# Gate and up products: three 256-column matmuls per block become one of 512 and one of 256 columns, and POOL takes two scalings and the last product

## The chip, the cores and the metric

The kernel runs on one core of a Trainium2 chip. The metric is the device time of one execution in microseconds (us). Each core has TensorE (PE; its weight loads are listed apart as PEld), VectorE (DVE), ScalarE (ACT), GpSimd (POOL) and SyncE (SP), which here only issues DMAs. Every engine works through its own queue in order, and an instruction that waits holds up all that stand behind it on that engine.

## The reference

Two layers of a decoder on x (256 tokens, 1024 features, float32). The change lies in the second half of a layer, the gated ConvFFN on RMSNorm(x):

```python
def conv_ffn(h, w_gate, w_up, conv_w, conv_b, w_down):   # h = rms_norm(x, ln2): [256, 1024]
    g = h @ w_gate                                        # w_gate, w_up: [1024, 2816]
    u = h @ w_up
    g = causal depthwise convolution of g, width 3, + conv_b
    return (silu(g) * u) @ w_down                         # w_down: [2816, 1024]
```

## The kernel before

Activations lie with features on the 128 partitions and the 256 tokens along the free axis. Float32 precision is kept by splitting: each operand is a high half and a low half (`hi`, `lo` for weights; `hTh`, `hTl` for h; `aTh`, `aTl` for the gated product), and a product is three matmuls in the function `mm3` (lines 195 to 197): high by high, high by low, low by high.

**Weights.** All weights pass through one stream in the order of their use. SP loads 1 MiB into a raw buffer; for each half MiB (a part) `split_next` puts a rounding copy on ACT (`hi`, line 180) and a subtraction on DVE (`lo`, line 181). Seven pairs of split buffers form a ring, and `weights()` keeps up to six parts split ahead of PE. So ACT and DVE do one `hi` and one `lo` for each part that PE uses, and a `hi` waits until PE has finished the part seven places earlier.

**The gate and up stage.** For each of NM = 22 blocks m of 128 hidden features, `products(m)` (line 849) computes gate and up: each has its own part of weights and, for 8 blocks k of the contraction, one `mm3` into a [128, 256] half of a PSUM bank. Banks come from the tags `acc` and `s`, two each, in turn; the block m = 2 uses `o` and `m` instead. `combine(m)` (line 858) then runs on the other engines, with R the norm's factor per token:

1. DVE: gr = gate x R (line 860)
2. ACT: y = conv tap 2 x gr + bias (line 862)
3. DVE: two `scalar_tensor_tensor` add the shifted taps to y (line 864)
4. ACT: s = Silu(y) (line 867)
5. POOL: s = s x R (line 868)
6. DVE: y = up x s (line 869), up still in PSUM
7. ACT: aTh = high half of y (line 870); DVE: aTl = the rest (line 871)

The blocks 0 and 1 are combined together behind the products of block 1, since R is computed (`norm2`, line 841) behind the products of block 0. After the stage, `down` (line 301) multiplies the 22 blocks by w_down; the blocks' results are used there in their order. Which instruction stands where on ACT, DVE and POOL is decided when the program is built, by a scheduler that fills each engine's queue; on the chip that order is fixed.

Of the kernel before, what the change touches and what calls it, by code (L numbers as in the profile page):

```python
# [11 lines left out]
F32 = mybir.dt.float32  # L12
# [8 lines left out]
P = 128  # L21
# [11 lines left out]
# steps of the attention behind each part of a chunk of the input projection, and of the output projection  # L33
# [3 lines left out]
# input projection: chunks of columns in the order in which they are computed  # L37
# [22 lines left out]
# rows of w_out in the order in which the pairs of heads are finished  # L60
# [4 lines left out]
# small per-layer parameters, [128, SMN]  # L65
O_LN1, O_LN2, O_CW, O_CB, O_PEK, O_PEV, SMN = 0, 8, 16, 82, 104, 120, 136
# gain rows
G_QA, G_KA, G_QB, G_KB1, G_KB2, G_QC, G_KC, G_KB0 = range(8)
# constants
# [41 lines left out]
def emit(ctx, tc, a):  # L111
# [22 lines left out]
    hTh = cst.tile([P, 8, S], F32R, name="hTh")  # L134
    hTl = cst.tile([P, 8, S], F32R, name="hTl")
# [7 lines left out]
    # ---- weights: streamed in the order of their use, each split into two 12-bit halves  # L143
    RAWN, SPN, AHEAD = 3, RING, RING - 1
    stream = []  # (source, columns of a part, parts): a part is half of a 1 MiB transfer
# [20 lines left out]
    after = []  # the splits are queued behind these  # L166
# [32 lines left out]
    def rsqrt(out, ss, n, tmp=None):  # L199
        # out = (ss / n + eps) ** -0.5  # L200
        v, w, q = tmp or [sml.tile(list(out.shape), F32, tag=f"rs_{i}", name=f"rs_{i}") for i in "vwq"]
        # a first value by exp(-0.5 ln v), then one step of Newton's method
        V.tensor_scalar(v, ss, 1.0 / n, EPS, ALU.mult, ALU.add)
        A.activation(out=w, in_=v, func=ACTF.Ln)
        A.activation(out=w, in_=w, func=ACTF.Exp, scale=-0.5)
        V.tensor_tensor(q, w, w, ALU.mult)
        V.scalar_tensor_tensor(q, q, -0.5, v, ALU.mult, ALU.mult)
        V.scalar_tensor_tensor(out, q, 1.5, w, ALU.add, ALU.mult)

    def make_h(k, gcol, sqs):  # L210
        # h = x * gain in two halves, without the factor r of the norm; sqs += squares
        g = gcol[:, k:k + 1]
        ins = [A.activation(out=hTh[:, k], in_=xT[:, k], func=ACTF.Copy, scale=g)]
        ins.append(V.scalar_tensor_tensor(out=hTl[:, k], in0=xT[:, k], scalar=g, in1=f(hTh[:, k]), op0=ALU.mult, op1=ALU.subtract))  # L214
        if sqs is not None:
            square(k, sqs)
        return ins

    def square(k, sqs):
        # sqs[0]: the sum of the squares of the tiles 0..k  # L220
# [7 lines left out]
    def factor(out, sqs, tag):  # L228
        # out[token, tile] = (sum of squares / D + eps) ** -0.5
# [6 lines left out]
    # keep the array's clock up while the first loads are under way  # L236
# [4 lines left out]
    # ---- the other loads, each behind a part of the stream  # L241
# [59 lines left out]
    def down(acc, lT, i0, i1, last, done=None, hold=False):  # L301
        # acc[d, tokens] += w^T lT for the parts i0..i1 of the contraction; two tiles of d share a bank
# [9 lines left out]
    for L in range(DEPTH):  # L312
        sm = sms[L]
        with ExitStack() as ph:
# [3 lines left out]
            # ---- the first norm: its factor r is applied to the rows of the projection  # L318
# [18 lines left out]
            def proj(c):  # L337
                # chunk c of the input projection, a part of the contraction at a time
# [21 lines left out]
            def qk_norm(q, groups):  # L360
                # rms norm and rope, in place, of the heads in q[:, t, 0:nh*64]; groups: (first head, heads, gain)
# [21 lines left out]
            def qk_T(z, outs_of):  # L383
                # -> for each group of heads, queries: [128, pair, head of pair, 256], each head's high halves on its own
                # rows (64 * head of pair ...) and its low halves on the other rows; keys: high halves on all rows,
                # [128, head of pair, pair, 256], and low halves on the head's own rows, [128, pair, 256]
# [30 lines left out]
            def qk_T32(z, h0, n, tag):  # L417
                # -> [128, pair, 256]: d of the two heads of a pair on rows 0..63 and 64..127
# [12 lines left out]
            def qk_mm(out, qs, p, k, t, kh, kl):  # L431
                # out = q k^T for the queries of tile t; kh, kl: [128, keys]
# [5 lines left out]
            def softmax(pr, ps, mask, m, nb, den):  # L438
                # pr[i] = exp(0.125 (ps[i] + mask[i] - max)), not normalised; m, nb, den: [P, 1] each
# [13 lines left out]
            def scores(pr, qT, kT, p, k, mk, m, nb, den):  # L453
                # pr: [P, 384] = (queries 0, keys 0), (queries 1, keys 0 and 1); m, nb, den: [P, 2]
# [6 lines left out]
            def scores2(qs, kk, p, k, m, nb, den):  # L461
                # selected and window keys at once: pr[:, branch]; m, nb, den: [P, 4] by (branch, tile)
# [11 lines left out]
            def prob_T(pr, sc):  # L474
                # pr: [P, 384] scaled by sc [P, 2] and transposed
# [5 lines left out]
                # columns: (keys 0, q 0) (keys 0, q 1) (keys 1, q 1)  # L481
# [4 lines left out]
            def pv(pTs, vs, O, first, last):  # L486
                # O[64 k.., q] += v^T p^T for the two heads k of a pair, on the two halves of the array at a time
# [28 lines left out]
            def attention():  # L516
                # the attention of all heads in steps; each yields the chunk of the projection that the next one needs
                yield 0
                gn = gns[L]
                # gains folded into the rope tables  # L520
# [10 lines left out]
                # ---- NSA: compressed keys and values  # L531
                hs = at.tile([P, 2, P], F32, tag="hs", name="hs", bufs=1)
                for i in range(2):
# [3 lines left out]
                    # t2[(parity, d), kv, s] = t[2 s + parity, kv, d]  # L537
# [15 lines left out]
                    # four column groups of the array at a time, each a part of the contraction  # L553
# [13 lines left out]
                # gelu, tanh form: z / (1 + exp(-2 sqrt(2 / pi) (z + 0.044715 z^3)))  # L567
# [12 lines left out]
                for i in range(2):  # L580
# [20 lines left out]
                    if i == 0:  # twice, for both halves of the queries  # L601
                        V.tensor_copy(b, bc(cb, [30, 2, HD]))
                    else:  # each of the two heads on its own columns
                        V.tensor_tensor(b, bc(cb, [30, 2, HD]), bc(bm, [30, 2, HD]), ALU.mult)
                    bd.append(b.rearrange("p h d -> p (h d)"))
                # values and, later, probabilities: high halves on rows 0..29; the high halves again or the low ones on 32..61
# [9 lines left out]
                # kc[:, k]: the high halves on all rows, the low halves on the rows of head k  # L616
# [18 lines left out]
                # compressed attention, all heads at once: [P, tile, pair, member, n]  # L635
# [20 lines left out]
                # gates: heads stand as (pair, member) = head pair + 3 * member  # L656
# [72 lines left out]
                # ---- dilated  # L729
# [12 lines left out]
                # weights of the groups: exp(m_g - M) / sum_g den_g exp(m_g - M)  # L742
# [13 lines left out]
                # ---- MoBA  # L756
# [59 lines left out]
            # ---- output projection  # L816
# [16 lines left out]
        with ExitStack() as ph:  # L833
# [7 lines left out]
            def norm2():  # L841
                # the second norm's factor, along the free dimension on all partitions
# [6 lines left out]
            def products(m):  # L849
                gu = [bank((("acc", "s"), ("o", "m"))[m == 2][i], "ps_gu")[:, :S] for i in range(2)]  # L850
                ws = [weights() for _ in range(2)]
                for ps, (hi, lo) in zip(gu, ws):
                    for k in range(8):
                        cs = slice(k * P, (k + 1) * P)
                        mm3(ps, hi[:, cs], lo[:, cs], hTh[:, k], hTl[:, k], k == 0, k == 7)
                return gu

            def combine(m, g, u):
                gr = ff.tile([P, S], F32, tag="gr", name="gr", bufs=3)
                V.tensor_tensor(gr, g, R, ALU.mult)  # L860
# [7 lines left out]
                G.tensor_tensor(s_, s_, R, ALU.mult)  # L868
                V.tensor_tensor(y, u, s_, ALU.mult)  # L869
# [3 lines left out]
            waiting = []  # L873
            for m in range(NM):
                waiting.append((m, *products(m)))
# [3 lines left out]
                if m >= 1:  # L879
                    for w in waiting:  # L880
                        combine(*w)
                    waiting = []
# [46 lines left out]
def build(arrays):  # L929
    nc = bacc.Bacc("TRN2", target_bir_lowering=False, num_devices=1)  # L930
# [12 lines left out]
```

## Time and profile before

| what | value |
|---|---|
| time, median of 3 runs | 679.56 us (679.25 to 679.63) |
| span of the profiled execution, first to last instruction | 677.8 us |
| the median less that span | 1.8 us |
| mean granted TensorE clock | 0.995 |
| busy: PE, PEld, DVE, ACT, POOL | 98%, 91%, 72%, 58%, 14% |

The profiled execution has its span alone; the median of the runs is 1.8 us longer, which is taken as what lies around a span. Busy time counts an instruction from its start to its end. Matmuls overlap each other, so the distance from one start to the next tells the pace, not the duration that is listed.

### The profile page before, as it was taken

What the parts mean: (1) busy time and instruction counts of PE and PEld (TensorE: products, weight loads), DVE (VectorE), ACT (ScalarE), POOL (GpSimd) and SP (SyncE); (2) the same over time, 40 slices, a digit from 0 to 9 for tenths busy, and PEclk for the clock granted to TensorE, in tenths of its full rate; (3) what the DMA queues carried; (4) which work ended last, traced back from release to release, by engine and by line L of the source; (5) the groups of instructions that cost most, each with busy time, mean ns of one, the idle gap of its engine ahead of it and who ended that gap; (6) DMA issues with size and microseconds to landing.
All of it is one profiled execution on the core that took longest, in us unless ns stands there. A gap on an engine that the chain in (4) does not pass through costs nothing. (4 is left out here: it accounts for less than half of the span.)

```text
span 677.8 us, 12841 instructions
## 1 busy us (share of the span) xinstructions
PE 665.2 (98%) x5062; PEld 617.0 (91%) x5062; DVE 488.0 (72%) x1066; ACT 396.4 (58%) x786; POOL 97.1 (14%) x133
## 2 busy tenths in 40 slices
PE   7999999999999999999989999999999999999997
PEld 6889768889999999999988887687999999999997
DVE  6689877769877777744476898796787777775432
ACT  5467779568555555543365767876765555555320
POOL 6301000112111111100050010010311111110000
PEclk9899999999999999999989999999999999999999
DMA  7956234515555555564745421533265555556501
GB/s 236 375 175 207 82 118 143 187 64 187 167 178 179 178 182 182 184 214 158 239 172 187 151 78 67 187 124 126 68 243 186 180 178 181 180 177 222 190 2 63
DMA packets 19356, 111.84 MB, mean 165 GB/s; under 512 B 2144, under 2 KB 3936, under 8 KB 8288
## 3 DMA queue, kind: packets, MB, share of 16 engines
q1 hardware_dynamic: 19296, 111.02, 48.5%
q8 instruction: 40, 0.66, 0.4%
q14 instruction: 20, 0.16, 0.1%
HBM read 109.97 MB, written 1.05 MB: 164 GB/s over the span
## 5 line engine op out<-in xcount | busy, mean ns | idle before, releaser
L181 DVE TENSOR_TENSOR lo<-raw,hi 128x1024 fp32r<-128x1024 f32 (+3 forms) x212 | 242.3, 1150 | 79.9 <-ACT hi L180 79.0
L180 ACT ACTIVATE hi<-raw 128x1024 fp32r<-128x1024 f32 (+3 forms) x212 | 207.8, 989 | 77.8 <-PE ps_dn L196 50.7
L195 PE MATMUL ps_gu<-hTh,hi 128*128 128x256 f32 x704 | 199.6, 284 | 0.0
L196 PE MATMUL ps_gu<-hTl,hi 128*128 128x256 f32 x704 | 199.4, 283 | 0.1
L197 PE MATMUL ps_gu<-hTh,lo 128*128 128x256 f32 x704 | 199.2, 283 | 0.0
L196 PEld LDWEIGHTS ps_gu<-hTl,hi 128*128 128x128 f32 x704 | 135.1, 192 | 0.5 <-DVE hTl L214 0.5
L195 PEld LDWEIGHTS ps_gu<-hTh,hi 128*128 128x128 f32 x704 | 135.1, 192 | 0.1
L197 PEld LDWEIGHTS ps_gu<-hTh,lo 128*128 128x128 f32 x704 | 135.1, 192 | 0.0
L195 PE MATMUL ps_dn<-aTh,hi 128*128 128x256 f32 x352 | 98.6, 280 | 0.0
L196 PE MATMUL ps_dn<-aTl,hi 128*128 128x256 f32 x352 | 98.2, 279 | 0.0
L197 PE MATMUL ps_dn<-aTh,lo 128*128 128x256 f32 x352 | 98.2, 279 | 0.0
L196 PE MATMUL ps_in<-lo,hTh 128*128 128x384 f32 (+3 forms) x256 | 90.6, 355 | 3.2 <-DVE lo L181 3.2
L195 PE MATMUL ps_in<-hi,hTh 128*128 128x384 f32 (+3 forms) x256 | 90.4, 356 | 0.2 <-ACT hi L180 0.2
L197 PE MATMUL ps_in<-hi,hTl 128*128 128x384 f32 (+3 forms) x256 | 89.4, 350 | 0.0
L197 PEld LDWEIGHTS ps_dn<-aTh,lo 128*128 128x128 f32 x352 | 66.2, 188 | 0.0
L195 PEld LDWEIGHTS ps_dn<-aTh,hi 128*128 128x128 f32 x352 | 66.1, 188 | 0.0
L196 PEld LDWEIGHTS ps_dn<-aTl,hi 128*128 128x128 f32 x352 | 65.8, 187 | 0.0
L196 PEld LDWEIGHTS ps_in<-lo,hTh 128*128 128x128 f32 x256 | 49.3, 193 | 8.3 <-DVE lo L181 4.4
L870 ACT CAST aTh<-cy 128x256 fp32r<-128x256 f32 x44 | 17.9, 407 | 65.7 <-DVE cy L869 65.6
L195 PEld LDWEIGHTS ps_in<-hi,hTh 128*128 128x128 f32 x256 | 49.0, 192 | 6.1 <-issue 2.8
L197 PEld LDWEIGHTS ps_in<-hi,hTl 128*128 128x128 f32 x256 | 49.4, 193 | 3.6 <-issue 1.2
L864 DVE SCALAR_TENSOR_TENSOR cy<-gr,sm,cy 128x255 f32<-128x255 f32 x88 | 42.1, 481 | 2.2 <-ACT cy L862 0.7
(316 smaller groups left out, 930.3 us busy)
## 6 DMA issues: line engine op xcount, KB each, us to landing
raw<-w_gu SPq DMA_DIRECT2D x44, 1024.0 KB, 5.0
raw<-w_down SPq DMA_DIRECT2D x22, 1024.0 KB, 4.8
raw<-w_in SPq DMA_DIRECT2D x16, 768.0 KB, 4.3
raw<-w_in SPq DMA_DIRECT2D x8, 1024.0 KB, 4.9
raw<-w_out SPq DMA_DIRECT2D x8, 1024.0 KB, 4.9
w<-cw SPq DMA_DIRECT2D x4, 1024.0 KB, 8.6
raw<-w_in SPq DMA_DIRECT2D x4, 512.0 KB, 3.7
raw<-w_in SPq DMA_DIRECT2D x4, 274.0 KB, 4.6
```

Source lines behind the costliest of these rows:

```text
L180: A.activation(out=hi[:, :n], in_=r, func=ACTF.Copy)
L181: V.tensor_tensor(out=lo[:, :n], in0=r, in1=f(hi[:, :n]), op=ALU.subtract)
L195: T.matmul(out, lhsT=lh, rhs=rh, start=start, stop=False, skip_group_check=skip)
L196: T.matmul(out, lhsT=lh, rhs=rl, start=False, stop=False, skip_group_check=skip)
L197: T.matmul(out, lhsT=ll, rhs=rh, start=False, stop=stop, skip_group_check=skip)
L864: V.scalar_tensor_tensor(out=y[:, j:], in0=gr[:, :S - j], scalar=cw[:, m, 2 - j:3 - j], in1=y[:, j:], op0=ALU.mult, op1=ALU.add)
L870: A.copy(aTh[:, m], y)
```

## The change

h's two halves move into one tile, so that for each block k the 256 high and the 256 low columns lie side by side. Each `mm3` of the stage becomes two matmuls: the weights' high half against all 512 columns, into both halves of a PSUM bank, and the low half against the 256 high columns, into the first half. For gate and for up, ACT copies the second half of the bank to SBUF, DVE adds the first half, and POOL multiplies by R. The last product y = up x s moves from DVE to POOL and reads SBUF alone; the old scaling of s on POOL goes. All blocks use the banks of `acc` and `s`, and each block is combined right behind its products. A new tile `cu` (three buffers) holds the up product; a scratch area for DMAs is made smaller to give it room.

```diff
-    hTh = cst.tile([P, 8, S], F32R, name="hTh")
-    hTl = cst.tile([P, 8, S], F32R, name="hTl")
+    hT = cst.tile([P, 8, 2, S], F32R, name="hT")
+    hTh, hTl = hT[:, :, 0], hT[:, :, 1]
...
             def products(m):
-                gu = [bank((("acc", "s"), ("o", "m"))[m == 2][i], "ps_gu")[:, :S] for i in range(2)]
+                gu = [bank(t, "ps_gu").rearrange("p (o n) -> p o n", o=2) for t in ("acc", "s")]
                 ws = [weights() for _ in range(2)]
                 for ps, (hi, lo) in zip(gu, ws):
                     for k in range(8):
                         cs = slice(k * P, (k + 1) * P)
-                        mm3(ps, hi[:, cs], lo[:, cs], hTh[:, k], hTl[:, k], k == 0, k == 7)
+                        T.matmul(ps, lhsT=hi[:, cs], rhs=hT[:, k], start=k == 0, stop=False, skip_group_check=True)
+                        T.matmul(ps[:, 0], lhsT=lo[:, cs], rhs=hTh[:, k], start=False, stop=k == 7, skip_group_check=True)
                 return gu
 
             def combine(m, g, u):
                 gr = ff.tile([P, S], F32, tag="gr", name="gr", bufs=3)
-                V.tensor_tensor(gr, g, R, ALU.mult)
+                uu = ff.tile([P, S], F32, tag="cu", name="cu", bufs=3)
+                for d, ps in ((gr, g), (uu, u)):
+                    A.copy(d, ps[:, 1])
+                    V.tensor_tensor(d, ps[:, 0], d, ALU.add)
+                    G.tensor_tensor(d, d, R, ALU.mult)
...
-                G.tensor_tensor(s_, s_, R, ALU.mult)
-                V.tensor_tensor(y, u, s_, ALU.mult)
+                G.tensor_tensor(y, uu, s_, ALU.mult)
                 A.copy(aTh[:, m], y)
                 V.tensor_tensor(aTl[:, m], y, f(aTh[:, m]), ALU.subtract)
 
-            waiting = []
             for m in range(NM):
-                waiting.append((m, *products(m)))
+                gu = products(m)
                 if m == 0:
                     after.clear()
                     norm2()
-                if m >= 1:
-                    for w in waiting:
-                        combine(*w)
-                    waiting = []
+                combine(m, *gu)
```

The queues change in the middle of the stage as follows. In the names, `cy` is y, `cs` is s, `cu` the up product, `ps_gu` the PSUM banks; line numbers of the change stand 1 to 6 higher. DVE, one block, before:

```order
L181 TENSOR_TENSOR lo<-raw,hi 128x1024 [waits Activation_49]
L864 SCALAR_TENSOR_TENSOR cy<-gr,sm,cy 128x255 [waits Activation_49]
L864 SCALAR_TENSOR_TENSOR cy<-gr,sm,cy 128x254 [waits DVE_49]
L181 TENSOR_TENSOR lo<-raw,hi 128x1024 [waits DMAHW7_49,PE_49,Activation_49]
L869 TENSOR_TENSOR cy<-ps_gu,cs__3084 128x256 [waits Pool_49]
L860 TENSOR_TENSOR gr<-ps_gu,R 128x256 [waits PE_49]
L871 TENSOR_TENSOR aTl<-cy,aTh 128x256 [waits Activation_49]
```

DVE, one block, in the change:

```order
L182 TENSOR_TENSOR lo<-raw,hi 128x1024 [waits PE_49,Activation_49]
L877 TENSOR_TENSOR aTl<-cy,aTh 128x256 [waits Activation_49]
L866 TENSOR_TENSOR gr<-ps_gu,gr 128x256
L182 TENSOR_TENSOR lo<-raw,hi 128x1024 [waits DMAHW1_49,PE_49,Activation_49]
L866 TENSOR_TENSOR cu<-ps_gu,cu 128x256 [waits Activation_49]
L871 SCALAR_TENSOR_TENSOR cy<-gr,sm,cy 128x255 [waits Activation_49]
```

The gate's read of PSUM (now the sum, line 866) stood ahead of aTl of the block before and now stands behind it; between it and the taps (line 871) now stand one `lo` and the up product's sum. ACT, from one Silu to the next, before:

```order
L867 ACTIVATE cs__3084<-cy 128x256 [waits DVE_49,Activation_49,Pool_49]
L870 CAST aTh<-cy 128x256 [waits DVE_49]
L180 ACTIVATE hi<-raw 128x1024 [waits PE_49]
L862 ACTIVATE cy<-gr,sm 128x256 [waits DVE_49]
L180 ACTIVATE hi<-raw 128x1024 [waits DMAHW0_49,PE_49]
L867 ACTIVATE cs__3156<-cy 128x256 [waits DVE_49,Activation_49,Pool_49]
```

ACT, in the change:

```order
L874 ACTIVATE cs__2969<-cy 128x256 [waits DVE_49,Activation_49]
L865 COPY gr<-ps_gu 128x256 [waits PE_49]
L876 CAST aTh<-cy 128x256 [waits Pool_49]
L181 ACTIVATE hi<-raw 128x1024 [waits DMAHW1_49,PE_49]
L865 COPY cu<-ps_gu 128x256 [waits PE_49]
L869 ACTIVATE cy<-gr,sm 128x256 [waits Pool_49]
L181 ACTIVATE hi<-raw 128x1024 [waits PE_49]
L874 ACTIVATE cs__3030<-cy 128x256 [waits DVE_49,Activation_49]
```

Two copies are new, and both the CAST and the first tap (line 869) now wait for POOL. POOL, in the change (before, one scaling of `cs` per block stood there):

```order
L867 TENSOR_TENSOR gr<-gr,R 128x256 [waits DVE_49]
L867 TENSOR_TENSOR cu<-cu,R 128x256 [waits DVE_49]
L875 TENSOR_TENSOR cy<-cu,cs__2969 128x256 [waits Activation_49,Pool_49]
L867 TENSOR_TENSOR gr<-gr,R 128x256 [waits DVE_49]
L867 TENSOR_TENSOR cu<-cu,R 128x256 [waits DVE_49]
L875 TENSOR_TENSOR cy<-cu,cs__3030 128x256 [waits Activation_49,Pool_49]
```

POOL goes from one to three operations for each block: gate by R, up by R, and the last product, which is the one that stands behind the Silu.

## Rows read from the trace of the kernel before

**Rows 1.** Busy by engine: us, share of the span, instructions (the page).

```profile
PE 665.2 (98%) x5062; PEld 617.0 (91%) x5062; DVE 488.0 (72%) x1066; ACT 396.4 (58%) x786; POOL 97.1 (14%) x133
```

**Rows 2.** Windows A:B: busy us by engine (count), granted clock, DMA share, GB/s.

```profile
200.00:260.00 60.00, 60.00 (x502) 60.00 (x501) 46.52 (x74) 33.16 (x52) 11.75 (x11) 1.00 0.54 179
60.00:90.00 30.00, 29.78 (x159) 22.83 (x159) 26.59 (x102) 23.11 (x64) 0.74 (x2) 1.00 0.31 102
```

**Rows 3.** Timeline of PE: start us, us, instruction; first and last of runs.

```profile
200.25 0.28 PE L195 MATMUL ps_gu<-hTh,hi 128*128 128x256 f32 x1
...
201.33 0.28 PE L195 MATMUL ps_gu<-hTh,hi 128*128 128x256 f32 x1
```

**Rows 4.** Timeline of PE in the input projection, 512-column matmuls, first and last.

```profile
38.53 0.39 PE L197 MATMUL ps_in<-hi,hTl 128*128 128x512 f32 x1
...
39.89 0.39 PE L197 MATMUL ps_in<-hi,hTl 128*128 128x512 f32 x1
```

**Rows 5.** Timeline of ACT over one block of the stage [idle before, releaser].

```profile
195.56 0.42 ACT L867 ACTIVATE cs__2436<-cy 128x256 f32<-128x256 f32 x1 [0.84 <-DVE cy L864]
...
197.67 0.41 ACT L870 CAST aTh<-cy 128x256 fp32r<-128x256 f32 x1 [1.69 <-DVE cy L869]
197.98 1.06 ACT L180 ACTIVATE hi<-raw 128x1024 fp32r<-128x1024 f32 x1
198.95 0.58 ACT L862 ACTIVATE cy<-gr,sm 128x256 f32<-128x256 f32 x1
...
201.33 0.42 ACT L867 ACTIVATE cs__2508<-cy 128x256 f32<-128x256 f32 x1 [0.85 <-DVE cy L864]
```

**Rows 6.** Timeline of DVE over the same block.

```profile
195.36 1.22 DVE L181 TENSOR_TENSOR lo<-raw,hi 128x1024 fp32r<-128x1024 f32 x1
...
197.21 0.42 DVE L869 TENSOR_TENSOR cy<-ps_gu,cs__2436 128x256 f32<-128x256 f32 x1 [0.63 <-POOL cs__2436 L868]
197.56 0.41 DVE L860 TENSOR_TENSOR gr<-ps_gu,R 128x256 f32<-128x256 f32 x1
198.11 0.42 DVE L871 TENSOR_TENSOR aTl<-cy,aTh 128x256 fp32r<-128x256 f32 x1
199.07 1.23 DVE L181 TENSOR_TENSOR lo<-raw,hi 128x1024 fp32r<-128x1024 f32 x1 [0.54 <-ACT hi L180]
200.22 1.00 DVE L864 SCALAR_TENSOR_TENSOR cy<-gr,sm,cy 128x255 f32<-128x255 f32 x2
```

**Rows 7.** Timeline of POOL: the same operation in that block, and earlier.

```profile
196.06 1.12 POOL L868 TENSOR_TENSOR cs__2436<-cs__2436,R 128x256 f32<-128x256 f32 x1 [4.64 <-ACT cs__2436 L867]
...
169.05 0.74 POOL L868 TENSOR_TENSOR cs__2076<-cs__2076,R 128x256 f32<-128x256 f32 x1
```

**Rows 8.** Timeline of DVE beside that second POOL row.

```profile
169.13 0.42 DVE L869 TENSOR_TENSOR cy<-ps_gu,cs__2064 128x256 f32<-128x256 f32 x1 [0.60 <-POOL cs__2064 L868]
```

**Rows 9.** Timelines of DVE and POOL elsewhere: one DVE form twice, POOL beside the second.

```profile
148.59 0.47 DVE L214 SCALAR_TENSOR_TENSOR hTl<-xT,sm,hTh 128x256 fp32r<-128x256 f32 x1
...
343.50 1.03 DVE L214 SCALAR_TENSOR_TENSOR hTl<-xT,sm,hTh 128x256 fp32r<-128x256 f32 x1 [1.67 <-ACT hTh L213]
...
342.69 1.56 POOL L224 TENSOR_TENSOR sqs<-sqs,xsq 128x256 f32<-128x256 f32 x2
```

**Rows 10.** Timeline of ACT: an evacuation of 128x256 from PSUM.

```profile
474.25 0.37 ACT L510 CAST oh<-ps_o 128x256 fp32r<-128x256 f32 x1 [0.97 <-PE ps_o L492]
```

**Rows 11.** Timelines of DVE and ACT at the start of layer 0's stage.

```profile
162.53 0.43 DVE L208 SCALAR_TENSOR_TENSOR R<-R_cs,R_cy 128x256 f32<-128x256 f32 x1
...
174.07 0.42 ACT L867 ACTIVATE cs__2148<-cy 128x256 f32<-128x256 f32 x1 [1.92 <-DVE cy L864]
```

**Rows 12.** Line 195's matmuls: count, ns min/median/max, first and last start.

```profile
L195 PE MATMUL ps_gu<-hTh,hi x704: 279/283/467, 152.4 to 611.7; 128*128 128x256 f32 x176
...
L195 PE MATMUL ps_dn<-aTh,hi x352: 280/280/282, 279.8 to 673.9; 128*128 128x256 f32 x176
```

More of the change, by code (lines that the diff above doesn't have):

```diff
@@ L929, in build @@
 def build(arrays):
-    nc = bacc.Bacc("TRN2", target_bir_lowering=False, num_devices=1)
+    nc = bacc.Bacc("TRN2", target_bir_lowering=False, num_devices=1, dynamic_dma_scratch_size=2048)
     a = {k: nc.dram_tensor(k, v.shape, F32, kind="ExternalInput").ap() for k, v in arrays.items()}
```

## The prediction

> **What bounds the kernel now.** Begin with the busy table [rows 1]: PE is busy 98% of the span, POOL 14%. It names PE, but it is an average, so the stage is looked at by itself. In 60 us of the stage [rows 2] PE and its weight loads are busy all 60 us at granted clock 1.00; PE waits for nobody there. From one line-195 matmul to the tenth after it, nine steps, pass 201.33 - 200.25 = 1.08 us [rows 3], so a 256-column matmul costs 0.120 us, and a block of 48 costs 5.76 us.
>
> A second view shows what the busy table hides. Follow one block through ACT, DVE and POOL, from Silu at 195.56 to the next Silu at 201.33, 5.77 us [rows 5, 6, 7]: Silu to POOL's start 0.50; POOL and y's start on DVE 1.15; CAST 0.46 later; hi 0.31; lo 1.09; the two taps 1.15 after lo's start; Silu 1.11 after theirs. These steps add up to 5.77, each released by the one before or by the engine coming free, and PE's products are in none of them. So the round of `combine` is a loop that takes 5.77 us by itself, as much as PE's block. It is a second bound, just hidden. A faster PE meets it at once, and a longer loop shows in full.
>
> **PE's part of the change.** 704 matmuls of 256 columns go, and 704 others become 512 wide. The nearest row for 512 columns is the input projection without transposes between: six steps in 39.89 - 38.53 = 1.36 us, 0.227 each [rows 4]. A block then costs 16 x (0.227 + 0.120) = 5.55 us, 0.21 less. If nothing else bound, 44 blocks would give 9.4 us. Where no row has the mixed sequence, the bounds are that a joined matmul saves nothing (0.240, no gain) and that the 256 beside it costs its columns alone (0.227 - 0.120 = 0.107 per 256 columns), 0.334 a pair and 18 us; 9.4 is the middle, and both rows have it.
>
> **The loop after the change**, along the new queues, from Silu at 0.
>
> - *y on POOL.* It stands where the old scaling stood, behind Silu and beside a lo, so it takes its time: start 0.50, end 1.62 [rows 7]. The same form without that neighbour takes 0.74 [rows 7], also beside a DVE operation that reads PSUM [rows 8]. The difference is a wait: the lo runs until 195.36 + 1.22 = 196.58, and POOL ends 0.60 after that [rows 6, 7].
> - *CAST* 1.66, *aTl* 2.10 (0.44 later), then the *gate's sum* 2.45 to 2.87: steps of 0.35 and a length of 0.42 from the DVE rows with a PSUM operand [rows 5, 6]. ACT's copies are 0.37 each [rows 10]; they stand behind Silu and hi where ACT has room (it now idles 0.84 and 1.69 in each block, [rows 5]), and cost nothing while that lasts. If ACT filled up they would cost 0.7 a block.
> - *Gate x R on POOL* 2.92 to 3.66, at 0.74. This is new on the path; before, DVE did it in 0.41 straight from PSUM.
> - *lo*. Its hi runs 1.97 to 3.03, so it is due at 3.05, while POOL is at work. DVE waits too when it comes second: the form of line 214 takes 0.47 alone and 1.03 beside POOL, whose pair of operations runs until 342.69 + 1.56 = 344.25; DVE ends 0.28 after that [rows 9]. A lo has four times those columns, so it ends 4 x 0.28 = 1.12 after POOL, at 4.78.
> - *Up's sum* 4.70 to 5.12, then the *first tap* 5.05 to 5.53 (half of 1.00, [rows 6]). The tap on ACT, 3.71 to 4.29, is ready before; so the taps are late by DVE's queue: lo and the up sum, moved ahead of them.
> - *Up x R on POOL* is due at 5.17, waits for the first tap, ends 0.60 behind it at 6.13. The *second tap* ends 0.28 later, 6.41; *Silu* at 6.52.
>
> So the loop becomes **6.52 us** where PE needs 5.55. Without any of these meetings of POOL and DVE, the same walk gives 5.27; with the one that the trace already shows in this place, 5.65. The ends for the unknown cost are therefore 5.27 and, with one more meeting of 0.28, 6.80; I take 6.52, since rows 7 and 9 show both directions of the wait at the same operand kinds (both operands in SBUF).
>
> A rule to weigh against rows 7: the Trainium skill (SBUF — State Buffer, Who interferes with whom) says that a DVE instruction with two SBUF inputs and a POOL instruction that reads SBUF exclude each other, and whichever is second waits for the whole of the other. By that, POOL would end a full 0.74 behind the lo and not 0.60; the trace shows the wait, but a little shorter. At three meetings the loop would be 0.4 longer and the time 13 us more.
>
> **What it costs.** Two banks each for gate and up mean that PE may start the gate of block m + 2 only after the gate's sum of block m. The stage starts with R, ready at 162.53 + 0.43 = 162.96 in layer 0 [rows 11]; POOL then has four scalings and the y of blocks 0 and 1 ahead of block 2. Two further POOL operations at 0.74 to 1.12 put block 2's Silu some 1.9 us behind today's 174.07 [rows 11], at 176.0. Block 18's Silu comes at 176.0 + 16 x 6.52 = 280.3, the gate's sum of block 19 ends at 283.2, and PE's last block, 5.55 long, at 288.8. Today `down` starts at 279.8 [rows 12]: 9.0 us later. PE's lead of two banks is spent by about block 6, and from there it waits some 0.97 us per block. The second layer's stage is the same, so 18.0 us in all. The span becomes 677.8 + 18.0 = 695.8, and with the 1.8 us between it and the median, 697.6 us.
>
> Edits costed at nothing: y leaves DVE and one sum comes, so DVE keeps its count. PSUM is read earlier in a block, which the missing third pair of banks for block 2 needs; if R's own work on ACT delayed the first copies, the two banks would be spent sooner, but the end is set by the loop. `down` finds six parts split (17 us of PE) when the stage ends, which covers the loop's tail. PE's pauses should not lower its clock: with weight loads busy 22.83 of 30 us it was granted 1.00 [rows 2].
>
> **Rivals.**
>
> 1. *PE stays the bound: faster.* If the meetings cost less than counted, the loop fits. The point is where 176.0 + 16 L + 2.92 + 5.55 equals 279.8: L = 5.96. Below 5.65, PE runs free: 679.6 - 9.4 = 670.2 us. For it: POOL did run in 0.74 beside DVE operations that read PSUM [rows 8], and two of DVE's seven per block are such sums. Against: lo, taps and aTl have two SBUF operands, and rows 7 and 9 show the wait. Chance 0.15.
> 2. *Some meetings miss each other.* Every 0.1 us of L is 3.2 us. With L from 5.65 to 6.2 the time lies between 670 and 687; within 0.2% of now (about what a measurement of this kernel can tell from no change) means L within 0.04 of 5.96. Chance 0.11, of which 0.04 no change, 0.03 faster, 0.04 slower.
> 3. *The fixed part of a matmul is small, so joining two saves nearly nothing.* The row for it would be a step near 0.107; the rows show 0.120 and 0.227, 13 ns above the columns' share in both, so I give it 0.01. The price would be 677.8 us and more where rival 1 holds; under the long loop it changes nothing. The Trainium skill (TensorE: Matmul & The Clock Gate, Back-to-back issue gap) has this rule: about 2.5 ns beside the columns. The trace here shows 13.
>
> The forecast, slower by the loop, has 0.73. Its own range is L from 6.2 to 6.8: 687 to 707 us.
>
> **How the numbers follow.** Slower 0.73 + 0.04 = 0.77; same 0.04 + 0.01 = 0.05; faster 0.15 + 0.03 = 0.18. The range for 8 in 10 takes the forecast's own and rival 2 down to L near 5.8, 674 to 707; rival 1's 670 stays out.
>
> **What would show it.** Right: POOL's three operations at over 0.74 on average, lo and the second tap longer than 1.22 and 0.48 where POOL runs, Silu to Silu about 6.5 us, and PE waiting for DVE's gate sum (line 866) some 0.9 us in each block from about the sixth, with ps_gu steps of 0.227 and 0.120 in between. Wrong: PE without waits in the stage at 5.55 us a block, or a wait on hi or lo, or a clock below 1.00 there.

## The result and the profile after

The change makes the kernel slower: 695.91 us (median of 4 runs, 694.69 to 697.42) against 679.40 us (4 runs on the same chip, 678.96 to 679.63), a ratio of 1.0248 with a 95% interval of 1.0229 to 1.0267. The profiled execution took 696.86 us, its span is 694.9 us where before it was 677.8, and its granted clock 0.998.

The page's busy line, after, which answers to [rows 1]:

```profile
PE 663.7 (96%) x4358; PEld 576.2 (83%) x4358; DVE 517.2 (74%) x1066; ACT 422.9 (61%) x874; POOL 171.8 (25%) x221
```

PE has 704 matmuls fewer, yet is busy only 1.5 us less, and DVE, with as many instructions as before, 29 us more. The same window of the stage as in [rows 2]:

```profile
200.00:260.00 60.00, 54.11 (x299) 45.43 (x299) 48.27 (x66) 36.08 (x66) 24.95 (x28) 1.00 0.48 170
```

PE, which waited for nobody here, now stands still for 5.9 of 60 us, at an unchanged clock of 1.00. One round of `combine` shows why. Timelines of DVE, ACT and POOL from one Silu to the next (start, us, instruction, idle before and releaser), which answer to [rows 5, 6, 7]:

```profile
203.04 1.22 DVE L182 TENSOR_TENSOR lo<-raw,hi 128x1024 fp32r<-128x1024 f32 x1
205.33 0.43 DVE L877 TENSOR_TENSOR aTl<-cy,aTh 128x256 fp32r<-128x256 f32 x1 [1.07 <-ACT aTh L876]
205.67 0.42 DVE L866 TENSOR_TENSOR gr<-ps_gu,gr 128x256 f32<-128x256 f32 x1
206.28 1.70 DVE L182 TENSOR_TENSOR lo<-raw,hi 128x1024 fp32r<-128x1024 f32 x1 [0.20 <-ACT hi L181]
207.91 0.41 DVE L866 TENSOR_TENSOR cu<-ps_gu,cu 128x256 f32<-128x256 f32 x1
208.24 1.35 DVE L871 SCALAR_TENSOR_TENSOR cy<-gr,sm,cy 128x255 f32<-128x255 f32 x2
```

```profile
203.22 0.42 ACT L874 ACTIVATE cs__2359<-cy 128x256 f32<-128x256 f32 x1 [1.20 <-DVE cy L871]
204.89 0.41 ACT L876 CAST aTh<-cy 128x256 fp32r<-128x256 f32 x1 [0.99 <-POOL cy L875]
206.94 0.60 ACT L869 ACTIVATE cy<-gr,sm 128x256 f32<-128x256 f32 x1 [0.43 <-POOL gr L867]
209.69 0.42 ACT L874 ACTIVATE cs__2420<-cy 128x256 f32<-128x256 f32 x1 [1.20 <-DVE cy L871]
```

```profile
203.78 1.08 POOL L875 TENSOR_TENSOR cy<-cu,cs__2359 128x256 f32<-128x256 f32 x1 [0.94 <-ACT cs__2359 L874]
206.17 0.74 POOL L867 TENSOR_TENSOR gr<-gr,R 128x256 f32<-128x256 f32 x1 [1.31 <-DVE gr L866]
208.40 0.92 POOL L867 TENSOR_TENSOR cu<-cu,R 128x256 f32<-128x256 f32 x1 [1.49 <-DVE cu L866]
```

From Silu to Silu pass 209.69 - 203.22 = 6.47 us; before it was 5.77. In three places POOL and DVE lie beside each other: y beside the end of a lo (1.08 instead of 0.74), gate x R beside the next lo (the lo takes 1.70 instead of 1.22), up x R beside the taps (1.35 for both instead of 1.00, and 0.92 on POOL).

PE meets this loop through the two PSUM banks of gate. PE and its weight loads where a block begins:

```profile
206.20 0.19 PEld L857 LDWEIGHTS ps_gu<-hT,hi 128*128 128x128 f32 x1 [0.96 <-ACT aTh L876]
206.24 0.47 PE L857 MATMUL ps_gu<-hT,hi 128*128 128x512 f32 x1 [0.67 <-DVE gr L866]
206.31 0.19 PEld L858 LDWEIGHTS ps_gu<-hT,lo 128*128 128x128 f32 x1
206.54 0.28 PE L858 MATMUL ps_gu<-hT,lo 128*128 128x256 f32 x1
...
206.66 0.40 PE L857 MATMUL ps_gu<-hT,hi 128*128 128x512 f32 x1
...
206.89 0.28 PE L858 MATMUL ps_gu<-hT,lo 128*128 128x256 f32 x1
```

The weight load starts behind the gate's sum (205.67 + 0.42 = 206.09); the CAST that its row names had long been done. The last three rows show the pace: 0.12 us from a 256-column matmul to the next of 512 columns, 0.23 from that to the next of 256.

### The profile page after: what moved, and what is told of

Same layout as the page of the kernel before. It is cut to its first block, busy times and chain, and to the rows that moved or that the text cites. A ratio compares the mean times of both kernels' runs of the same rounds, so it can differ in the third digit from the quotient of the medians.

```text
span 694.9 us, 11692 instructions
## 1 busy us (share of the span) xinstructions
PE 663.7 (96%) x4358; PEld 576.2 (83%) x4358; DVE 517.2 (74%) x1066; ACT 422.9 (61%) x874; POOL 171.8 (25%) x221
## 5 line engine op out<-in xcount | busy, mean ns | idle before, releaser
L857 PE MATMUL ps_gu<-hT,hi 128*128 128x512 f32 x704 | 250.5, 399 | 19.2 <-DVE gr L866 18.8
L858 PE MATMUL ps_gu<-hT,lo 128*128 128x256 f32 x704 | 196.4, 279 | 0.0
L857 PEld LDWEIGHTS ps_gu<-hT,hi 128*128 128x128 f32 x704 | 132.0, 188 | 58.5 <-ACT aTh L876 27.6
L858 PEld LDWEIGHTS ps_gu<-hT,lo 128*128 128x128 f32 x704 | 132.7, 188 | 0.1
L197 PE MATMUL ps_in<-lo,hT 128*128 128x384 f32 (+3 forms) x256 | 89.9, 352 | 3.1 <-DVE lo L182 3.1
L196 PE MATMUL ps_in<-hi,hT 128*128 128x384 f32 (+3 forms) x256 | 89.9, 354 | 0.4 <-ACT hi L181 0.4
L198 PE MATMUL ps_in<-hi,hT 128*128 128x384 f32 (+3 forms) x256 | 88.6, 347 | 0.0
L867 POOL TENSOR_TENSOR cu<-cu,R 128x256 f32<-128x256 f32 x44 | 41.7, 948 | 56.8 <-DVE cu L866 56.8
L197 PEld LDWEIGHTS ps_in<-lo,hT 128*128 128x128 f32 x256 | 48.7, 190 | 8.2 <-DVE lo L182 4.2
L196 PEld LDWEIGHTS ps_in<-hi,hT 128*128 128x128 f32 x256 | 48.4, 190 | 6.4 <-issue 2.8
L198 PEld LDWEIGHTS ps_in<-hi,hT 128*128 128x128 f32 x256 | 48.7, 190 | 3.6 <-issue 1.2
L867 POOL TENSOR_TENSOR gr<-gr,R 128x256 f32<-128x256 f32 x44 | 33.1, 751 | 68.7 <-DVE gr L866 49.8
```

Of the source, the lines that this page charges most:

```text
L196: T.matmul(out, lhsT=lh, rhs=rh, start=start, stop=False, skip_group_check=skip)
L197: T.matmul(out, lhsT=lh, rhs=rl, start=False, stop=False, skip_group_check=skip)
L198: T.matmul(out, lhsT=ll, rhs=rh, start=False, stop=stop, skip_group_check=skip)
L857: T.matmul(ps, lhsT=hi[:, cs], rhs=hT[:, k], start=k == 0, stop=False, skip_group_check=True)
L858: T.matmul(ps[:, 0], lhsT=lo[:, cs], rhs=hTh[:, k], start=False, stop=k == 7, skip_group_check=True)
L867: G.tensor_tensor(d, d, R, ALU.mult)
```

## The experiments

The theory is the prediction's: reads of SBUF by POOL and by DVE operations with two SBUF operands wait for each other, these waits lie on the combine loop, and PE waits for the loop. The rivals are that the loop is longer because POOL is one more station in it, that ACT and DVE are simply fuller, or that the last product on POOL alone does it. Times are medians, and ratios are against runs of the kernel before on the same chip. The third column is from the profiled executions: a stage runs from its first `ps_gu` matmul to the first `ps_dn` one, and the column gives the two stages' sum less the 254.8 us of before. Comments in the diffs are added here.

| run | Silu to Silu, us | both stages, us | time, us | ratio, 95% interval |
|---|---|---|---|---|
| the change | 6.46 | +19.1 | 695.91 | 1.0248 [1.0229, 1.0267] |
| no_r | 5.64 | -8.8 | 668.87 | 0.9836 [0.9817, 0.9855] |
| mset | 5.64 | -8.8 | 669.48 | 0.9855 [0.9838, 0.9872] |
| b_read (from before) | 6.13 | +10.5 | 689.94 | 1.0152 [1.0125, 1.0179] |
| b_write (from before) | 5.77 | 0.0 | 679.41 | 0.9995 [0.9983, 1.0007] |
| rg_dve | 6.17 | +8.1 | 683.66 | 1.0066 [1.0046, 1.0087] |
| pipe | 6.00 | +2.0 | 679.50 | 0.9997 [0.9984, 1.0010] |
| y_dve | 5.80 | -5.1 | 670.77 | 0.9866 [0.9841, 0.9891] |
| up_only | 5.98 | -1.6 | 675.91 | 0.9947 [0.9929, 0.9965] |
| hand | 5.32 | -6.7 | 669.15 | 0.9848 [0.9824, 0.9872] |

### no_r: without the two multiplies

```diff
                     A.copy(d, ps[:, 1])
                     V.tensor_tensor(d, ps[:, 0], d, ALU.add)
-                    G.tensor_tensor(d, d, R, ALU.mult)
```

> The changed kernel without the two multiplies by R on POOL, in each block (the norm factor R is left out of the result; all else stays). Theory (POOL's operations and DVE's two-input SBUF operations wait for each other, and this lengthens the combine loop): y still meets one lo, so the loop is about 5.65 us from Silu to Silu; that is below the decisive 5.96, PE then runs at its 5.55 to 5.65 a block without a wait for DVE, the lo's fall back to 1.22 us and the two taps to 1.00, and the time is 670 us, at most 673. Rival (it is not POOL but the two copies on ACT and the sum more on DVE that fill these engines): the loop stays over 6.2 and the time over 687.

The loop is 5.64 us and the time 668.87 us. PE runs all 60 us of the window:

```profile
200.00:260.00 60.00, 60.00 (x348) 52.42 (x347) 46.59 (x75) 39.68 (x74) 11.52 (x11) 1.00 0.55 188
```

So the copies on ACT and the sums on DVE, which are all still there, are not the cost; the two multiplies are. It does not yet say whether by their place in the chain or by their reads.

### mset: the same chain, without POOL's reads

```diff
-                    G.tensor_tensor(d, d, R, ALU.mult)
+                    for _ in range(2):
+                        G.memset(d, 1.0)
```

> The changed kernel, with each of the two multiplies by R on POOL replaced by two memsets of the same tile (0.36 us each in the run with junk memsets, so 0.73 together where the multiply alone takes 0.74; the norm factor and the data of both halves are left out of the result). The chain sum, POOL, tap on ACT stays, with the same time on POOL; only POOL's reading of SBUF is gone. Theory (the wait for each other on SBUF is what made the loop longer): the lo behind the gate's sum takes 1.22, the two taps 1.00, loop 5.68, time 669 to 673 us. Rival (POOL as one more station in the chain, 0.74 us and a semaphore for gate and up, is the cost): loop 6.2 to 6.5, time 687 to 697.

This is the run that decides. POOL, and then DVE, in one round:

```profile
220.34 1.07 POOL L876 TENSOR_TENSOR cy<-cu,cs__2625 128x256 f32<-128x256 f32 x1 [0.83 <-ACT cs__2625 L875]
222.70 0.68 POOL L868 MEMSET gr<- 128x256 f32 x2 [1.29 <-DVE gr L866]
224.45 0.69 POOL L868 MEMSET cu<- 128x256 f32 x2 [1.07 <-DVE cu L866]
```

```profile
222.84 1.23 DVE L182 TENSOR_TENSOR lo<-raw,hi 128x1024 fp32r<-128x1024 f32 x1 [0.20 <-ACT hi L181]
223.98 0.42 DVE L866 TENSOR_TENSOR cu<-ps_gu,cu 128x256 f32<-128x256 f32 x1
224.31 0.99 DVE L872 SCALAR_TENSOR_TENSOR cy<-gr,sm,cy 128x255 f32<-128x255 f32 x2
```

POOL still stands between the sums and what follows, for 0.68 us, and it writes SBUF beside the lo and beside the taps; both are back at 1.23 and 0.99. The loop is 0.83 us shorter than the change's (5.64 for 6.46, rounded), and that is 0.48 of the lo (1.70 - 1.22) and 0.36 of the taps (1.35 - 0.99). The station in the chain costs nothing here: the lo and up's sum ahead of them on DVE, not the tap on ACT, are what the taps wait for.

### b_read and b_write: junk beside the kernel before

```diff
                 G.tensor_tensor(s_, s_, R, ALU.mult)
+                jk = ff.tile([P, S], F32, tag="jk", name="jk", bufs=1)
+                for _ in range(4):                                    # b_write: 8
+                    tc.keep_in_program_order(G.tensor_tensor(jk, R, R, ALU.mult))   # b_write: G.memset(jk, 0.0)
```

> The kernel before, with four POOL multiplies R x R into a tile that nobody reads, in each block directly behind its s x R (the result is unchanged by them). Nothing waits for them but POOL's own next scaling. Theory: they read SBUF beside the lo, the last product, aTl and the taps, so these and the junk wait for each other; about 0.56 to 0.6 us more in a round or more: loop 6.3 to 7.0 where it was 5.77, and the time 697 to 720 us. Rival (POOL and DVE don't hinder each other here; 1.12 us was only the duration of that form): POOL is busy some 4.1 of 5.77 us, nothing is late, 679.5 us.

> The kernel before, with eight POOL memsets of a tile that nobody reads in place of the four multiplies (about 0.3 us each by half of the 512-column memset's 0.53, so some 2.4 us of POOL per block; they read nothing; the result is unchanged). Theory (it is reading SBUF that makes the two wait): loop 5.77 as before, time 679 to 681. Rival (any work on POOL beside DVE slows it, or the s x R is simply later because POOL is busy): over 685, with longer lo's and taps.

The memsets kept POOL busy for 36.10 of the 60 us window (11.75 before), and nothing moved. The reads cost 1.5%, some 10 us: the mechanism holds without any of the change's other parts. But the size was missed: 689.94 us, below the expected 697 to 720. DVE and POOL in one round of b_read:

```profile
222.05 0.61 DVE L874 TENSOR_TENSOR aTl<-cy,aTh 128x256 fp32r<-128x256 f32 x1
223.01 1.23 DVE L181 TENSOR_TENSOR lo<-raw,hi 128x1024 fp32r<-128x1024 f32 x1 [0.35 <-ACT hi L180]
224.16 1.35 DVE L864 SCALAR_TENSOR_TENSOR cy<-gr,sm,cy 128x255 f32<-128x255 f32 x2
...
221.08 3.64 POOL L871 TENSOR_TENSOR jk<-R 128x256 f32<-128x256 f32 x4
```

The expectation counted a wait on the lo too. Here the lo went first and the junk waited; aTl grew by 0.19, but the lo behind it waited for hi (0.35) anyway. What is left on the path is the taps' 0.35, and the loop grew by nearly just that, from 5.77 to 6.13.

### rg_dve: gate x R on DVE

```diff
-                    G.tensor_tensor(d, d, R, ALU.mult)
+                    (V if d is gr else G).tensor_tensor(d, d, R, ALU.mult)
```

> The changed kernel with gate x R on DVE, directly behind the gate's sum; up x R and the last product stay on POOL. POOL then no longer stands in front of the lo, but DVE does 0.42 us more. Walk from Silu at 0: y 0.50 to 1.67, CAST 1.71, aTl 2.16, gate's sum 2.50, gate x R 2.96 to 3.38, lo 3.30 to 4.52, up's sum 4.44, first tap 4.78, up x R 4.90 to 5.86 between the taps, second tap until 6.14, Silu 6.23. Theory: loop 6.23, time 695.9 - 32 x (6.465 - 6.23) = 688 us (684 to 692), taps still over 0.6 on average and lo back at 1.22. Rival (the chain through POOL is the cost): with one station less the loop is 5.5 to 5.7, 669 to 673.

The loop is 6.17 us, the lo took 1.22 and the pair of taps 1.35. The station is gone and the time is still above that of before, so the rival's 669 to 673 is out. The ten runs go from 680.66 to 686.98, wider than those of the other kernels; the median lies just under the expected 684. In the profiled execution, the shortest of the ten, the stages took 8.1 us more than in before, but `down` took 59.7 us in both layers where before it took 62.1 (last section), which gives 4.7 back.

### y_dve: the last product back on DVE

```diff
-                G.tensor_tensor(y, uu, s_, ALU.mult)
+                V.tensor_tensor(y, uu, s_, ALU.mult)
```

> The changed kernel with the last product (up times Silu) back on DVE, the two multiplies by R on POOL. The order on DVE becomes y, gate's sum, aTl, up's sum, lo, two taps, lo, and on ACT up's copy comes ahead of the first hi. Walk from Silu at 0: the lo ahead runs until 1.07, y 0.99 to 1.41, gate's sum 1.33 to 1.75, CAST 1.50, gate x R 1.79 to 2.53, aTl 1.95 to 2.81 behind it, up's sum 2.73, up x R 3.19 to 3.93, lo 3.21 waits until 5.00, taps 4.92 to 5.92, Silu 6.01. Theory: loop 6.01, time about 681 us (677 to 686); the lo's that follow up x R 1.6 to 1.8 us. Rival (y on POOL alone is what the change costs, the multiplies are cheap): loop under 5.7, 670.

The time is the rival's (670.77 us), the loop nearly the theory's (5.80 for 6.01), and the miss is instructive. DVE and POOL:

```profile
225.11 0.96 DVE L877 TENSOR_TENSOR aTl<-cy,aTh 128x256 fp32r<-128x256 f32 x1
225.99 0.41 DVE L866 TENSOR_TENSOR cu<-ps_gu,cu 128x256 f32<-128x256 f32 x1
226.34 1.22 DVE L182 TENSOR_TENSOR lo<-raw,hi 128x1024 fp32r<-128x1024 f32 x1
...
226.55 1.61 POOL L867 TENSOR_TENSOR cu<-cu,R 128x256 f32<-128x256 f32 x1 [0.77 <-DVE cu L866]
```

The walk had up x R ahead of the lo, which would then have been late until 5.00. DVE's lo started first, and POOL waited for it instead (1.61), off the path. That the multiplies are cheap, as the rival says, is not so: gate x R stretches aTl to 0.96 and up x R the taps to 1.48. But a loop of 5.80 loses only 0.25 a block to PE's 5.55, so PE's lead of two banks lasts long: in the second layer PE's blocks take 5.55 us up to block 14 and 5.76 to 5.80 in the blocks 15 to 20, and in the first they take 5.65 and PE does not wait. Of the 8.6 us by which the profiled span is shorter than before, the stages give 5.1; `down` in the first layer gives 2.3, and a clock that did not fall between the stages 1.6 (last section for both), which no walk had. That the time met the rival's 670 is in part luck.

### pipe: the same work, emitted in another order

`combine` is written as two functions, and the second half of block m - 1 is emitted behind the first half of block m:

```diff
-                combine(m, *gu)
+                late.append(part_a(m, *gu))   # copies, sums, multiplies by R, tap on ACT
+                if m >= 1:
+                    part_b(*late.pop(0))      # taps, Silu, last product, aTh, aTl
```

> The changed kernel with the combine step written in two parts, the sums, multiplies and the tap on ACT of block m + 1 ahead of the taps, Silu and last product of block m; the operations and their engines are the same. In the steady blocks only two things change place: the gate's copy stands ahead of Silu on ACT, and the gate's sum ahead of aTl on DVE, so gate x R runs 0.9 us earlier, beside CAST. Walk: gate's sum 0.99 to 1.41, gate x R 1.63 to 2.37, lo 3.11 to 4.33 free, up's sum 4.25, taps 4.59 to 5.95 with up x R between them, Silu 6.04. Theory: loop 6.04, time about 682 us (677 to 687). Rival (order does not matter, the engines are simply full): 6.4 and 694 or more.

The loop is 6.00 us where 6.04 was expected, and the time 679.50, no different from before (the two stages take 2.0 us more). That is the prediction's point of decision (a loop of 5.96 gives no change), met by an experiment. Gate x R ran in 0.74 beside CAST and the lo took 1.23; the meetings of y with a lo (1.08) and of up x R with the taps (1.35) are left.

### up_only: half of the change

```diff
-                gu = [bank(t, "ps_gu").rearrange("p (o n) -> p o n", o=2) for t in ("acc", "s")]
+                gu = [bank("acc", "ps_gu")[:, :S], bank("s", "ps_gu").rearrange("p (o n) -> p o n", o=2)]
...
+                        if i == 0:
+                            mm3(ps, hi[:, cs], lo[:, cs], hTh[:, k], hTl[:, k], k == 0, k == 7)
+                            continue
...
-                for d, ps in ((gr, g), (uu, u)):
-                    A.copy(d, ps[:, 1])
-                    V.tensor_tensor(d, ps[:, 0], d, ALU.add)
-                    G.tensor_tensor(d, d, R, ALU.mult)
+                V.tensor_tensor(gr, g, R, ALU.mult)
+                A.copy(uu, u[:, 1])
+                V.tensor_tensor(uu, u[:, 0], uu, ALU.add)
+                G.tensor_tensor(uu, uu, R, ALU.mult)
```

> Half of the change: 512-column products, two banks, sum and multiply on POOL for up alone; the gate's products in three matmuls of 256 columns as before, its multiply by R on DVE straight from PSUM; the last product on POOL. PE: 8 x (0.2267 + 0.120) + 24 x 0.120 = 5.65 us a block. POOL has two operations per block in place of three. Theory: without gate x R, POOL's two operations lie beside the up sum, the gate's multiply (PSUM operand) and one lo, not beside the taps; a walk over the new queues gives 5.65, PE's own pace, so PE bound: 44 x 0.105 = 4.6 us less, 675 us (673 to 677). Rival (what the change costs is the last product on POOL and the copies): loop over 6.0, 681 or more.

The time is as expected, 675.91 us, but by luck. The stages give 1.6 us of the 4.6 that were forecast, because a block takes PE 5.71 us and not 5.65, and the blocks 1 and 2 take 5.88; another 2.5 us come from the stretch between the stages, where PE waited 1.0 us less than in before and the clock did not fall (last section). That PE is the bound is so: it is busy all 60 us of the window. The loop was missed: 5.98 us. DVE and POOL:

```profile
223.08 1.65 DVE L182 TENSOR_TENSOR lo<-raw,hi 128x1024 fp32r<-128x1024 f32 x1
...
223.72 1.60 POOL L878 TENSOR_TENSOR cy<-cu,cs__2669 128x256 f32<-128x256 f32 x1
```

A lo waits for up x R (1.65) and y for the end of that lo (1.60), so two meetings stand one behind the other in front of CAST; the walk had up x R earlier and so one. It reaches PE only in the last block, where a weight load waits 0.2 us for up's sum: the loop falls back by 0.27 a block, some 5 us over the stage, about as much as PE's lead.

### hand: the same operations, the order written out

```diff
+            pin = tc.keep_in_program_order
...
+                for d, ps in ((gr, g), (uu, u)):        # sums(m)
+                    pin(A.copy(d, ps[:, 1]))
+                    pin(V.tensor_tensor(d, ps[:, 0], d, ALU.add))
...
+                pin(G.tensor_tensor(last[1], last[2], last[3], ALU.mult))   # y of m - 1
+                for d in (gr, uu):
+                    pin(G.tensor_tensor(d, d, R, ALU.mult))
+                split(m)                                # hi, lo
+                finish(*last[:2])                       # aTh, aTl of m - 1
...
+                split(m)                                # hi, lo, behind the taps of m
```

> The changed kernel with the same operations on the same engines, but the order of a block's work on ACT, DVE and POOL written out: both copies from PSUM ahead of the first hi, both sums ahead of the first lo, the two multiplies by R behind y on POOL, aTl and the taps behind the lo. So y, gate x R and up x R stand one after the other beside the two sums (PSUM operand) and one lo, and POOL and DVE meet about once per block in place of three times. Theory: the same walk gives a loop of about 5.3 us, below PE's 5.55: PE bound, no waits for DVE in the stage, time 670 us (668 to 673), faster than both kernels. Rival 1 (it is the amount of work on the three engines, not its order): loop stays over 6.2, time over 687. Rival 2 (meetings only move): loop 5.7 to 6.1, 672 to 684.

669.15 us, 1.5% faster than before and 27 us below the change, with the same operations on the same engines. One round on POOL, then on DVE:

```profile
210.72 1.08 POOL L880 TENSOR_TENSOR cy<-cu,cs__2487 128x256 f32<-128x256 f32 x1 [1.85 <-ACT cs__2487 L893]
211.77 0.73 POOL L882 TENSOR_TENSOR gr<-gr,R 128x256 f32<-128x256 f32 x1
212.46 1.72 POOL L882 TENSOR_TENSOR cu<-cu,R 128x256 f32<-128x256 f32 x1
```

```profile
209.98 1.22 DVE L182 TENSOR_TENSOR lo<-raw,hi 128x1024 fp32r<-128x1024 f32 x1
211.12 0.42 DVE L869 TENSOR_TENSOR gr<-ps_gu,gr 128x256 f32<-128x256 f32 x1
211.45 0.42 DVE L869 TENSOR_TENSOR cu<-ps_gu,cu 128x256 f32<-128x256 f32 x1
212.11 1.48 DVE L182 TENSOR_TENSOR lo<-raw,hi 128x1024 fp32r<-128x1024 f32 x1 [0.24 <-ACT hi L181]
213.51 0.96 DVE L898 TENSOR_TENSOR aTl<-cy,aTh 128x256 fp32r<-128x256 f32 x1
214.39 0.99 DVE L889 SCALAR_TENSOR_TENSOR cy<-gr,sm,cy 128x255 f32<-128x255 f32 x2
```

POOL's three operations follow one another. The waits have not gone (up x R takes 1.72, the lo 1.48, aTl 0.96); in place of the one meeting per block that was expected, four operations are lengthened, y among them. But y ends at 211.80, 0.60 behind the lo's 211.20, as in the change, although both sums, which read PSUM, run beside it; gate x R then starts ahead of the next lo and takes 0.73; and the taps, which end the loop, are free of POOL (0.99). The loop is 5.32 us, below PE's 5.55, and the list of waits has none of PE for a sum in this stage.

## Why the prediction was right

Predicted were 697.6 us (674 to 707) and slower with 0.77; measured 695.91. The first matmul of `down` after the change, which answers to [rows 12]:

```profile
L196 PE MATMUL ps_dn<-aTh,hi x352: 279/279/284, 289.5 to 690.9; 128*128 128x256 f32 x176
```

By the prediction's own steps:

- **The hidden second bound.** The loop of 5.77 us in the kernel before shows in full as soon as it is lengthened: b_read leaves PE's part alone, lengthens it by 0.36, and the time grows by 1.5%.
- **PE's pace.** The 512-column matmul starts 0.23 us ahead of the 256-column one, and that 0.12 ahead of the next. The blocks 2 to 4, before PE's lead is spent, take 5.55 us, as forecast from [rows 3, 4]. Rival 3 (a joined matmul saves nearly nothing) is out.
- **The gain if nothing else bound.** 670.2 us was given for rival 1; no_r, mset and hand, in which PE is free, measured 668.87, 669.48 and 669.15. In the stages themselves no_r and mset give 8.8 us for the 9.4 forecast; the rest of their gain lies outside them.
- **The walk.** From Silu at 0, forecast and measured: y's end 1.62 and 1.64, CAST 1.66 and 1.67, aTl 2.10 and 2.11, gate's sum 2.45 and 2.45, gate x R's end 3.66 and 3.69, lo's end 4.78 and 4.76, up's sum 4.70 and 4.69, end of the taps 6.41 and 6.37, Silu 6.52 and 6.47. The bound with y's meeting alone, 5.65, is answered by no_r and mset at 5.64; that without any, 5.27, no run in this order shows. How long a lo goes on behind POOL was a guess by columns, 4 x 0.28 = 1.12; measured is 206.28 + 1.70 - 206.91 = 1.07.
- **Which way the wait goes.** The rule of the Trainium skill (SBUF — State Buffer, Who interferes with whom) that was weighed there would have put POOL's end 0.74 behind the lo's and the loop at 6.9. Measured is y's end at 204.86, 0.60 behind the lo's 204.26, as in [rows 6, 7], and 6.47. The same section says that a DVE instruction with two SBUF inputs does not contend with a POOL instruction that only writes SBUF; mset and b_write agree (lo 1.23 beside a memset).
- **The sum.** Block 2's Silu came at 176.86 (176.0 forecast), and the first `ps_dn` matmul at 289.53 in place of 279.81: 9.7 us for 9.0; in the second layer 629.11 for 612.07, less the 7.54 us by which its stage begins later, 9.5. Together 19.2 us for 18.0. Two terms were short: block 2's start by 0.9 us, and the round of block 3, 6.97 in place of 6.52; the 15 rounds up to block 18, at 6.46, give 0.8 of it back. PE's last block in layer 0 took 5.72 for 5.55. The span grew by 17.1 only, because 2.2 us come back between the stages, which no step of the prediction had: 0.6 by a shorter wait, and 1.6 by a clock that fell in the profiled execution of before and not in that of after (last section). So it is partly luck that the total came so near.
- **PE's waits.** From block 6 on, as forecast, a block takes 6.46 us, a wait of 0.91 where 0.97 was said. The clock there stayed at 1.00, as said, but the row given for it ([rows 2], weight loads busy 22.83 of 30 us) does not bear on it: PE itself was busy 29.78 of those 30 us, so it shows next to no pauses.
- **The point of decision.** 5.96 us and 32 us of time per us of loop were forecast. The run pipe stands at 6.00 with no change; between it and the change lie 16.4 us of time and 0.46 us of loop, 35 per us. The slope goes on below the point, as rival 2 had it: the stage of layer 1 took 136.9 us at a loop of 6.46 (the change), 128.4 at 6.00 (pipe), 124.5 at 5.80 (y_dve) and 123.0 at 5.64 (mset), where PE is free.

What rival 1 had for it, that DVE operations that read PSUM leave POOL alone, is what [rows 7, 8] and hand show. The prediction took the built order of the queues as given, and for this kernel it was; the experiments show that the loss belongs to that order.

## What to carry to other kernels

Before making the bound engine faster, walk one round of the loop that feeds it on the other engines and add up the steps: here a second bound of the same length lay behind the first. Moving an operation to an idle engine is not free if it reads SBUF there beside DVE's two-operand operations; look at which instructions will stand beside it, put POOL's reads next to DVE operations with a PSUM operand, and keep them off the operations that end the loop. When a change makes the right engine faster and still loses, write out the order of the queues before giving up the change. And check a forecast in the stretch that the change works on: the total of up_only came out as expected although its stages gave a third of what was forecast.

## What the runs showed of the hardware that was not expected

**Who goes first decides what a meeting costs.** Of the same pair of operations, one direction lengthens the loop and the other is hidden: in the change POOL's gate x R went first and the lo took 1.70, in y_dve the lo went first, took 1.22, and POOL's up x R 1.61. A walk over the queues did not foresee this order each time: it missed y_dve's loop by 0.21 and up_only's by 0.33.

**A fall of the clock that comes in some executions.** Between the stages PE waits for POOL's sum of squares, in before and in after:

```profile
348.97 0.60 PE L233 MATMUL ps_ss<-ones,sqs 128*128 128x1 f32 x4 [2.24 <-POOL sqs L224]
```

```profile
358.11 0.61 PE L234 MATMUL ps_ss<-ones,sqs 128*128 128x1 f32 x4 [1.66 <-POOL sqs L225]
```

Windows behind it, of before and then of after (granted clock third from the end):

```profile
348.00:352.00 4.00, 3.03 (x19) 3.03 (x20) 3.40 (x6) 1.34 (x4) 0.92 (x1) 0.85 0.99 412
352.00:356.00 4.00, 4.00 (x19) 4.00 (x18) 3.35 (x6) 3.23 (x6) 0.00 (x0) 0.72 0.73 266
```

```profile
356.00:360.00 4.00, 2.34 (x19) 2.12 (x18) 4.00 (x6) 1.89 (x4) 1.97 (x2) 1.00 0.95 363
```

In before PE stood for 2.24 us, and its clock then fell from the higher of its two levels (2.4 GHz) to the lower (1.2 GHz): 0.15 of one window and 0.28 of the next, 4 us each, are 1.7 us of full clock lost, which is 3.4 us at half clock. In after it stood for 1.66 us and the clock stayed. That stretch, from the first `ps_dn` matmul of layer 0 to the first `ps_gu` one of layer 1, took 204.85 us before and 202.68 after.

Neither the change nor the length of the wait decides whether it falls. In the other profiled executions the clock fell behind the same wait in b_read, b_write, mset, pipe and hand (waits of 1.84, 2.01, 1.47, 1.35 and 2.64 us), and stayed at 1.00 in no_r, rg_dve, y_dve and up_only (1.69, 2.16, 2.26 and 1.24). From the last `ps_dn` matmul to the first `ps_gu` one, less this wait, pass 138.9 to 139.0 us where the clock stayed and 140.5 where it fell (142.1 in b_read, where it was down for longer), so a fall costs 1.5 to 1.6 us. With the shorter wait (0.58) that is the 2.2. What does decide it is open, and why POOL's sum was waited for a shorter time was not tried.

**PE's pace is not one number.** In hand and y_dve the blocks of layer 0 (from block 2) took 5.65 us without a wait, and `down` behind them 59.7 us; in layer 1, and in no_r and mset in both layers, the same blocks took 5.55 and `down` 62.1, at a granted clock of 1.00 in both. There the two nearly cancel in the time. In rg_dve they do not: `down` took 59.7 in both layers, and the blocks 2 to 6, before PE's lead is spent, took 5.55. Nor in up_only, where a pair of 512 and 256 columns takes 0.353 us, as in the blocks of 5.65 (16 pairs; 0.347 in those of 5.55), and `down` took 62.1. What sets this is open.
